# Sixteen modulation columns as one-column products on TensorE instead of VectorE reductions

## The chip, the core and the metric

The kernel runs on one core of one Trainium2 chip. The time is device microseconds of that core, as the median of three runs. In the profile PE is TensorE's matmuls, PEld its weight loads, DVE VectorE, ACT ScalarE, POOL GpSimd and SP the SyncE queue that issues the DMAs. Every engine works through its own instructions strictly in the order in which they stand there; a wait at the head of an engine's order holds everything behind it.

## The reference

Two layers and a large second block, on 512 tokens of 1024 features, all in fp32. What matters here is the modulation and the first layer, a convolution mixer:

```python
s_lat = jax.nn.silu(c)
for i in range(DEPTH):
    sh, sc, gt = jnp.split((s_lat @ w_mod[i] + b_mod[i])[:, None, :], 3, axis=-1)
    h = _rms(x, norm_g[i]) * (1.0 + sc) + sh
    ...
    x = x + gt * o

def _conv_mixer(h, w_in, dw, db, ln_g, ln_b, w_out):
    a, b, g = jnp.split(h @ w_in, 3, axis=-1)
    y = a * jax.nn.sigmoid(b)
    y = depthwise convolution of y with 31 taps + db
    y = jax.nn.silu(_layernorm(y, ln_g, ln_b)) * jax.nn.silu(g)
    return y @ w_out
```

The modulation is a product of one vector of 1024 numbers (silu of c) with matrices; the kernel makes 96 columns of 128 results of it. Columns 0 to 15 (shift and scale of layer 0) are needed before the first projection, 16 to 23 (its gate) and 24 to 31 (shift of layer 1) only after the convolution.

## The kernel before

x is kept feature-major: 8 chunks of 128 features by 512 tokens. Every large weight is split into hi + lo parts of a reduced fp32 type; a product of a 128x128 block with a chunk is three matmuls (`mm3`). Weights come in groups of 8 blocks (512 KB); for each group ScalarE casts hi (`whi`) and VectorE subtracts for lo (`wlo`, line 296).

The convolution stage runs from about 80 to 250 us. Its order on PE, ACT, DVE and POOL is written out by hand in the string `PLAN`: `l` is a chunk of the input projection (24 matmuls of 512 columns), `x` the sigmoid and product that follow it (VectorE makes the hi and lo tiles `e` for TensorE), `e` a step of the convolution on TensorE (12 matmuls of 256 columns with diagonals `dg`), `v` a step on VectorE (two operations, line 573), `p` a step on GpSimd (ScalarE multiplies by a tap, GpSimd adds), `b` makes diagonals (GpSimd, VectorE, or eight small ScalarE operations, line 525), `c` ends a chunk, and `g` is one column of the modulation. Chunks 0 and 2 are convolved on VectorE, 1 on GpSimd, 3 to 7 on TensorE.

A column is made by `gemv`: the 128x1024 slice `gw` comes by DMA into one of two buffers, and one VectorE operation (line 255) multiplies it by silu(c), which `cb` holds on every partition, and sums along the row into a column of `mod`; a small operation that reads the accumulator follows. The weight slice's buffer is free for the next DMA when VectorE has read it. PSUM banks of the pool `psr` (`pr()`, two banks) hold the last two results of the first projection (`r`), and later the mean and the statistics.

The first 16 columns are made before and during the first eight chunks of the projection (`lin_k`, until 79.7 us); the `g` of `PLAN` then make columns 16 onward, one after another.

Of the kernel before, what the change touches and what calls it, by code (L numbers as in the profile page):

```python
# [9 lines left out]
F32 = mybir.dt.float32  # L10
F32R = mybir.dt.float32r
AF = mybir.ActivationFunctionType
ALU = mybir.AluOpType

P = 128
T = 512
D = 1024
KC = D // P
# [11 lines left out]
# columns of the vector table  # L30
# [24 lines left out]
# how the work of the convolution is shared and ordered; with a count or a chunk, and the engines:  # L55
# l a chunk of the input projection, x what follows it, e v p a step of the convolution on TensorE, VectorE, GpSimd,
# b diagonals for TensorE's, c the end of a chunk, s a step of the statistics, z its norm, y its gate,
# m a source chunk of the output projection, g a column of the modulation
# [10 lines left out]
# steps of TensorE that a part of a stick-breaking head waits for the one before  # L69
# [20 lines left out]
# the projections of the stick-breaking heads in their order  # L90
# [3 lines left out]
def in2(name, i):  # L94
    """blocks of a part of the mixers' input projection"""
    if name == "v":
        return wide(SBV + 2 * i, 2)
    if name in "qk":
        return blocks_m_major(((SBQ if name == "q" else SBK) + i,), K8)
    if name == "rqk":  # L100
        return blocks_m_major((RQ + 2 * i, RQ + 2 * i + 1, RK + 2 * i, RK + 2 * i + 1), K8)
    if name == "rv":
        return wide(RV + 4 * i)
    if name == "rg":
        return blocks_m_major(range(RG + 4 * i, RG + 4 * i + 4), K8)
    return blocks_m_major(range(BRS, BRS + 16), K8)


# every block of every weight in the order of its use
# [17 lines left out]
# steps of TensorE at which a crossing emits its parts, per norm  # L127
# [4 lines left out]
def body(ctx: ExitStack, tc, ap, out):  # L132
    nc = tc.nc
# [15 lines left out]
    # working tiles of a phase, by tag  # L149
# [40 lines left out]
    # ---------------- constants  # L190
    vec = const.tile([P, NVEC], F32, name="vec")
    crow = gst.tile([P, D], F32, tag="g", name="crow")[0:1, :]
    ident = const.tile([P, P], F32, name="ident")
    x = []
    with tc.high_priority(offset=20000):
        for k in range(KC):
            t = const.tile([P, T], F32, name=nm("x"))
            nc.sync.dma_start(out=t, in_=ap["xt"][k])
            x.append(t)
            if k == 0:  # L200
                nc.sync.dma_start(out=crow, in_=ap["c"])
        nc.sync.dma_start(out=vec[:, 0:NHEAD], in_=ap["vec"][:, 0:NHEAD])
        nc.sync.dma_start(out=ident, in_=ap["cst"][:, 0:P])

# [20 lines left out]
    # 1 + b for the scales  # L225
    b1 = const.tile([P, 32], F32, name="b1")

    # mod columns: 0..23 layer 0 (shift, scale+1, gate), 24..47 layer 1, 48..95 second block
# [15 lines left out]
    def gemv():  # L244
        i = done[0]
        if i >= 96:
            return
        done[0] += 1
        if i == 48:
            cb.append(silu_c("c_2"))  # L250
        j = MOD_ORDER[i]
        with tc.high_priority(offset=3000):
            t = gst.tile([P, D], F32, tag="g", name=nm("gw"))
            nc.sync.dma_start(out=t, in_=ap["wmod"][j])
        product = V.tensor_tensor_reduce(  # L255
            out=t, in0=t, in1=cb[-1], scale=1.0, scalar=bias_of(j),
            op0=ALU.mult, op1=ALU.add, accum_out=mod[:, j:j + 1])
        tc.keep_in_program_order(product)
# [5 lines left out]
    # ---------------- weights  # L264
    at_block, loaded, fetched, groups, lead, ahead = [0], [0], [], {}, [LEAD], [0]

    def fetch(n):
        """ask for the groups up to the n-th"""
        while len(fetched) <= min(n, len(BLOCKS) // GB - 1):
            w = wst.tile([P, GB * P], F32, tag="w", name=nm("w"))  # L270
            with tc.high_priority(offset=3000):
                nc.sync.dma_start(out=w, in_=ap["weights"][len(fetched)])
            fetched.append(w)
# [6 lines left out]
    def group_steps(g, engs=None):  # L280
        """a group of blocks as hi + lo, with the next ones under way; a stop before lo"""
        while loaded[0] <= min(max(g, min(g + lead[0], at_block[0] // GB + 2)), len(BLOCKS) // GB - 1):
            n = loaded[0]
            loaded[0] += 1
            for _ in range(pace[0]):
                gemv()
            fetch(n + ahead[0])
            w, fetched[n] = fetched[n], None
            hi = wsp.tile([P, GB * P], F32R, tag="hi", name=nm("whi"))
            lo = wsp.tile([P, GB * P], F32R, tag="lo", name=nm("wlo"))  # L290
            A.copy(out=hi, in_=w)  # L291
            yield
            es = engs or (V if n else G,)
            for e, i in zip(es, range(0, GB * P, GB * P // len(es))):
                part = slice(i, i + GB * P // len(es))
                e.tensor_tensor(out=lo[:, part], in0=w[:, part], in1=f(hi[:, part]), op=ALU.subtract)  # L296
            groups[n] = hi, lo
            del w

    def block(i, n=1):  # L300
        """n blocks from the i-th after the current one"""
        g, r = divmod(at_block[0] + i, GB)
        hi, lo = group(g)
        return hi[:, r * P:(r + n) * P], lo[:, r * P:(r + n) * P]
# [15 lines left out]
    def lin(src, ms, kn, evac, halves=False, acc=acc):  # L320
        """feature-major products, one out-chunk after another"""
# [17 lines left out]
    def lin_k_steps(src, ms, kn, evac, banks=None):  # L339
        """k outermost, for sources that come one by one"""  # L340
# [24 lines left out]
    def split(src, scale=None, into=None, tag="a"):  # L365
        """PSUM as hi + lo"""
# [9 lines left out]
    def split_in(t, a=0, b=T, into=None, eng=None, n=T, tag="a"):  # L376
        """a tile as hi + lo"""
# [5 lines left out]
    # ---------------- statistics over features, per token  # L383
    class Stat:
        """sum of tiles"""
# [4 lines left out]
        def add(self, t):  # L390
            """the first tile is summed into"""
# [7 lines left out]
    def colsum(ps, c0, tiles, a, b, first=True, last=True):  # L399
        """ps[:, c0 + j] = sum over partitions and tiles of block j"""  # L400
# [5 lines left out]
    def bcast(ps, r, a, b):  # L406
        """ps[:, t] = r[t] on every partition; r has a token block in each column"""
# [3 lines left out]
    def rsqrt_steps(c, sq, n, a, b, rb, begun=False):  # L411
        """broadcast of 1/sqrt(mean + eps) into rb[:, a:b], with a stop before and after the root"""
# [10 lines left out]
    class Norm:  # L423
        """rms norm and modulation of x into split h, fed as chunks of x are updated"""
# [20 lines left out]
        def sum_half(self, m, a, b):  # L445
            """some tokens of a chunk into the sum"""
            V.tensor_tensor(out=self.sum.acc[:, a:b], in0=self.sum.acc[:, a:b], in1=self.tail[m][:, a:b], op=ALU.add)

        def sum_late(self):
            """all whole chunks into one sum"""  # L450
# [4 lines left out]
        def steps(self, a, b, early=False):  # L455
            """the statistics of some tokens"""
# [11 lines left out]
        def make_steps(self, k, a, b, pool=False):  # L468
            """a chunk of the result, with a stop before what waits for hi"""
# [18 lines left out]
        def makes(self, a, b):  # L488
            """all chunks, one after another"""
# [15 lines left out]
    # ================= first block, layer 0: convolution mixer  # L505
    # the taps of the chunks that TensorE convolves as hi | lo, and a diagonal per half of the partitions
# [10 lines left out]
    def diagonals(i, g, n, engs):  # L517
        """eight taps of 64 channels as hi and lo"""
# [44 lines left out]
    def conv_vector(chunks):  # L563
        """a tap of each chunk at a time"""
# [11 lines left out]
    def conv_pool(i):  # L576
        """a tap at a time"""
# [10 lines left out]
    def conv_tensor(i):  # L588
        """even and odd tokens of 64 channels on the two halves of the partitions, a few taps at a time"""
# [80 lines left out]
    def layer_stats():  # L670
        """mean and 1/sqrt(var + eps) of the convolved chunks, on every partition"""
# [49 lines left out]
    def crossing(which, src, ev, norm, half, free, *tiles):  # L721
        """the last two chunks of a residual and the first chunks of what follows its norm, by halves of the tokens"""
# [50 lines left out]
        # hi of a chunk, then its lo some chunks later; one result after another ends  # L773
# [25 lines left out]
    with tc.manual_schedule(engines=HAND):  # L799
# [33 lines left out]
        lead[0], ahead[0] = LEAD, 1  # L833
        engine = {"V": V, "A": A, "G": G}
# [38 lines left out]
    # ================= first block, layer 1: pooling mixer  # L873
# [7 lines left out]
    def pool_chunk(m, v):  # L881
        w = WINDOWS[m // 2]
        # running sums over aligned windows; v is padded by 8 in front and 8 behind
# [56 lines left out]
    # ================= second block: mixers  # L940
    h = n2.h
    # which score blocks share a PSUM bank: (block, offset, width)
# [5 lines left out]
    def lin_in(m):  # L948
        """one chunk of the mixers' input projection in two steps"""
# [8 lines left out]
    def sb_lin(w):  # L958
        i = int(w[1:])
        if w[0] == "v":  # L960
            # two pairs of heads, tokens on partitions: hi and lo of a head side by side
# [18 lines left out]
    # work that is emitted some steps of TensorE later  # L980
# [30 lines left out]
    def sb_q(i, o):  # L1011
        """per head hi and lo on the two halves of the partitions"""
# [7 lines left out]
    def sb_k(i, o):  # L1020
        """per head hi on both halves; lo of both heads"""
# [22 lines left out]
    def sb_scores(hd):  # L1044
# [20 lines left out]
        def softplus():  # L1065
            """softplus of the scores, summed over the later key blocks"""
# [61 lines left out]
    # retention: queries and keys of a head, chunk by chunk  # L1128
# [73 lines left out]
    # retention  # L1202
# [11 lines left out]
    def lin_tok():  # L1214
        """token-major products of 512 columns: four blocks of 128 tokens"""
# [77 lines left out]
    def ev_br(m, o, a, b):  # L1293
# [4 lines left out]
        else:  # L1298
            # all of the merged result but the last head
# [57 lines left out]
    # ================= feed-forward  # L1357
# [66 lines left out]


# ---- layout of the inputs
# [23 lines left out]
def taps_by_half(dw, db):  # L1450
    """taps and bias of the chunks that TensorE convolves, for even and odd tokens on the halves of the partitions"""
# [9 lines left out]
def arrays_of(i):  # L1461
# [4 lines left out]
    wm = np.concatenate([i["w_mod"][0].T, i["w_mod"][1].T, i["w_ada_2"][0].T], 0).reshape(96, P, D)  # L1466
    a["wmod"] = np.ascontiguousarray(wm)
# [30 lines left out]
```

## Time and profile before

| | us |
|---|---|
| runs, median of 3 | 1689.4 (1686.88 to 1690.16) |
| profiled execution, its span | 1686.7 |
| PE busy over the span | 1611.0 (96%) |
| DVE busy over the span | 1034.9 (61%) |
| ACT / POOL busy over the span | 596.0 / 500.8 |

The page gives no time of the profiled execution but its span; the median of the runs lies 2.7 us above it. Busy time is a share over stages with different limits: VectorE, at 61% of the whole, is in the convolution stage the busiest engine of all. A matmul's record is longer than its turn, since matmuls are pipelined; the distance from the start of one to the start of the next is what it costs in a row of them.

### The profile page before, as it was taken

The page shows a single profiled execution, that of the slowest core. Times are in us where ns is not written, and L with a number is a line of the kernel's source. Part 1 is how long each engine was busy: PE and PEld are TensorE (multiplying, and loading weights), DVE is VectorE, ACT ScalarE, POOL GpSimd, SP SyncE. Part 2 cuts the span into 40 slices and gives each one's busy share as a digit, 9 for nine tenths or more (in the row PEclk, how much of TensorE's full clock was granted, in tenths as well). Part 3 has the DMA queues.
Part 4 walks back from the last instruction along what each step waited for, and adds up shares of the span by engine and source line. Part 5 has one row for each costly group of instructions (what it writes and reads, how often), then busy time and mean ns, then how long its engine had stood idle before and what let it go on. Part 6 is the DMA issues. An engine that isn't in the chain of part 4 may idle for free.

```text
span 1686.7 us, 20261 instructions
## 1 busy us (share of the span) xinstructions
PE 1611.0 (96%) x7904; PEld 1347.1 (80%) x7904; DVE 1034.9 (61%) x1449; ACT 596.0 (35%) x920; POOL 500.8 (30%) x370
## 2 busy tenths in 40 slices
PE   6888899989999999999999999999999999999997
PEld 4677787867888878878888888888888888888887
DVE  6899987796677887886476554633254533333222
ACT  3422543513365556532332213223333422222221
POOL 2758645571124544460030200204441100000001
PEclk9999999999999999999999999999999999999999
DMA  7541334247521111225546332222322322332221
GB/s 266 168 150 64 113 126 147 74 148 250 187 76 51 60 53 51 70 66 158 175 144 201 99 119 75 94 89 75 99 91 84 100 90 99 100 100 90 98 92 58
DMA packets 54578, 187.64 MB, mean 111 GB/s; under 512 B 6097, under 2 KB 8273, under 8 KB 54482
## 3 DMA queue, kind: packets, MB, share of 16 engines
q1 hardware_dynamic: 52498, 183.20, 33.4%
q10 hardware_dynamic: 1984, 3.15, 0.6%
q8 instruction: 62, 1.02, 0.2%
q14 instruction: 34, 0.28, 0.1%
HBM read 184.22 MB, written 2.10 MB: 110 GB/s over the span
## 4 chain that ended last, share of the span: by engine, by line
PE 68%; DVE 18%; ACT 4%; issue 3%; DMA 3%; POOL 3%; SPq 0%; POOLq 0%; DVEq 0%; ACTq 0%
PE m L307 9%; PE m L309 9%; PE m L308 9%; PE z L309 7%; PE z L307 7%; PE z L308 7%; DVE wlo L296 4%; DVE gw L255 3%; DVE d L573 2%; DMA gw<-in_wmod 1%; DVE dg L527 1%; DMA w<-in_weights 1%; PE m L1222 1%; PE z L1222 1%; PE m L1224 1%
## 5 line engine op out<-in xcount | busy, mean ns | idle before, releaser
L296 DVE TENSOR_TENSOR wlo<-w,whi 128x1024 fp32r<-128x1024 f32 (+1 forms) x243 | 330.6, 1363 | 345.7 <-ACT whi L291 344.8
L291 ACT CAST whi<-w 128x1024 fp32r<-128x1024 f32 x244 | 255.2, 1049 | 633.2 <-PE m L308 269.9
L307 PE MATMUL m<-h,whi 128*128 128x512 f32 x730 | 287.4, 394 | 4.1 <-ACT a L644 2.0
L309 PE MATMUL m<-h,wlo 128*128 128x512 f32 x730 | 286.0, 392 | 3.5 <-DVE y L902 2.9
L308 PE MATMUL m<-h,whi 128*128 128x512 f32 x730 | 285.1, 391 | 1.9 <-POOL h L480 1.9
L309 PEld LDWEIGHTS m<-h,wlo 128*128 128x128 f32 x730 | 137.5, 188 | 34.1 <-DVE y L902 3.3
L307 PEld LDWEIGHTS m<-h,whi 128*128 128x128 f32 x730 | 137.9, 189 | 32.4 <-ACT a L644 2.2
L308 PEld LDWEIGHTS m<-h,whi 128*128 128x128 f32 x730 | 137.9, 189 | 29.8 <-POOL h L480 2.2
L309 PE MATMUL z<-h,wlo 128*128 128x512 f32 x338 | 133.0, 394 | 5.5 <-DVE y L902 5.4
L308 PE MATMUL z<-h,whi 128*128 128x512 f32 x338 | 132.8, 393 | 0.0
L307 PE MATMUL z<-h,whi 128*128 128x512 f32 x338 | 132.8, 393 | 0.0
L397 POOL TENSOR_TENSOR c<-c,c 128x512 f32<-128x512 f32 x10 | 13.4, 1337 | 372.9 <-ACT c L435 372.7
L397 POOL TENSOR_TENSOR s<-s,s 128x512 f32<-128x512 f32 x14 | 18.7, 1336 | 321.0 <-ACT s L1262 292.2
L255 DVE CUSTOM_DVE_ANT_0 gw<-gw,cb,vec 128x1024 f32<-128x1024 f32 x64 | 92.0, 1444 | 17.9 <-DMA gw<-in_wmod 11.4
L1041 POOL TENSOR_TENSOR s<-s,s 128x512 fp32r<-128x512 f32 x64 | 92.7, 1458 | 30.7 <-DVE s L1040 29.2
L309 PE MATMUL z<-a,wlo 128*128 128x512 f32 (+1 forms) x222 | 81.7, 368 | 1.5 <-DVE wlo L296 1.5
L307 PE MATMUL z<-a,whi 128*128 128x512 f32 (+1 forms) x222 | 82.1, 370 | 0.0
L308 PE MATMUL z<-a,whi 128*128 128x512 f32 (+1 forms) x222 | 81.5, 367 | 0.0
L309 PEld LDWEIGHTS z<-h,wlo 128*128 128x128 f32 x338 | 64.2, 190 | 20.2 <-DVE y L902 6.3
L308 PEld LDWEIGHTS z<-h,whi 128*128 128x128 f32 x338 | 64.0, 189 | 13.1
L307 PEld LDWEIGHTS z<-h,whi 128*128 128x128 f32 x338 | 64.1, 190 | 12.9
L307 PE MATMUL m<-a,whi 128*128 128x512 f32 (+1 forms) x196 | 71.5, 365 | 0.0
(415 smaller groups left out, 3540.2 us busy)
## 6 DMA issues: line engine op xcount, KB each, us to landing
w<-in_weights SPq DMA_DIRECT2D x244, 512.0 KB, 3.7
gw<-in_wmod SPq DMA_DIRECT2D x96, 512.0 KB, 4.2
x<-in_xt SPq DMA_DIRECT2D x8, 256.0 KB, 5.1
s<-in_dec ACTq DMA_DIRECT2D x4, 256.0 KB, 3.5
out_x<-h SPq DMA_DIRECT2D x4, 256.0 KB, 2.5
p<-in_cnt ACTq DMA_DIRECT2D x2, 256.0 KB, 2.7
v<-in_cnt ACTq DMA_DIRECT2D x2, 256.0 KB, 3.1
cb<-in_c SPq DMA_DIRECT2D x1, 512.0 KB, 6.1
```

Source lines behind the costliest of these rows:

```text
L255: product = V.tensor_tensor_reduce(out=t, in0=t, in1=cb[-1], scale=1.0, scalar=bias_of(j), op0=ALU.mult, op1=ALU.add, accum_out=mod[:, j:j ...
L291: A.copy(out=hi, in_=w)
L296: e.tensor_tensor(out=lo[:, part], in0=w[:, part], in1=f(hi[:, part]), op=ALU.subtract)
L307: mm(o, l[0], r[0], start=first, stop=False)
L308: mm(o, l[0], r[1], start=False, stop=False)
L309: mm(o, l[1], r[0], start=False, stop=last)
L397: self.eng.tensor_tensor(out=n, in0=self.acc, in1=t, op=ALU.add)
L527: engs[s].tensor_tensor(out=t.rearrange("p (a b) -> p a b", a=8), in0=diag.unsqueeze(1).to_broadcast([P, 8, P // 2]), in1=dws[s][:, c:c + ...
L573: V.scalar_tensor_tensor(out=cv[i], in0=y[:, j:j + T], scalar=tap(i, j), in1=cv[i], op0=ALU.mult, op1=ALU.add)
L1041: G.tensor_tensor(out=lo[:, 0:w], in0=t[:, 0:w], in1=f(hi[:, 0:w]), op=ALU.subtract)
L1222: mm(o, hh, wh, start=k == 0, stop=False)
L1224: mm(o, hl, wh, start=False, stop=k == KC - 1)
```

## The change

The slices of columns 16 to 31 are laid out anew in memory, so that a slice is eight 128x128 blocks with the input features on the partitions. Each of these columns is now eight fp32 matmuls of one moving column into a bank of `psr`, and a ScalarE operation that adds the bias and writes the column of `mod`. The vector c as a 128x8 tile (`ccol`) comes by one more DMA at the start, and ScalarE takes its silu after the first projection. The 16 VectorE reductions and their 16 accumulator reads fall away; the other 80 columns stay as they were.

```diff
+    ccol = const.tile([P, KC], F32, name="ccol")
...
         nc.sync.dma_start(out=ident, in_=ap["cst"][:, 0:P])
+        nc.sync.dma_start(out=ccol, in_=ap["ccol"])
...
     def gemv():
...
             nc.sync.dma_start(out=t, in_=ap["wmod"][j])
+        if j in MOD_ON_PE:
+
+            o = pr()
+            for k in range(KC):
+                mm(o[:, 0:1], t[:, k * P:(k + 1) * P], ccol[:, k:k + 1], start=k == 0, stop=k == KC - 1)
+            A.activation(out=mod[:, j:j + 1], in_=o[:, 0:1], func=AF.Identity, bias=bias_of(j))
+            return
         product = V.tensor_tensor_reduce(
...
         lin_k(h0, CV_FIRST, KC, ev_in)
         lead[0], ahead[0] = LEAD, 1
+        A.activation(out=ccol, in_=ccol, func=AF.Silu)
...
+MOD_ON_PE = set(range(16, 32))
...
+    a["ccol"] = np.ascontiguousarray(a["c"].reshape(KC, P).T)
+    for j in MOD_ON_PE:
+        wm[j] = wm[j].reshape(P, KC, P).transpose(2, 1, 0).reshape(P, D)
```

The orders of DVE, POOL and, apart from the new products, PE are the same as before; VectorE only loses 32 rows. On PE the place that matters first is the end of the first projection (`r` its last bank, `m` the bank of the next projected chunk). Before:

```order
L307 MATMUL r_233<-h_550,whi_521 128x512
L308 MATMUL r_233<-h_551,whi_521 128x512
L309 MATMUL r_233<-h_550,wlo_522 128x512
L307 MATMUL m_648<-h_206,whi_567 128x512
L308 MATMUL m_648<-h_207,whi_567 128x512
L309 MATMUL m_648<-h_206,wlo_568 128x512
```

And now, where each of the two new rows stands for eight products:

```order
L318 MATMUL r_235<-h_552,wlo_524 128x512
L261 MATMUL r_642<-ccol,gw_640 128x1 x8
L261 MATMUL r_659<-ccol,gw_657 128x1 x8
L316 MATMUL m_669<-h_208,whi_569 128x512
L317 MATMUL m_669<-h_209,whi_569 128x512
L318 MATMUL m_669<-h_208,wlo_570 128x512
```

The first two columns stand ahead of the first chunk of `PLAN`, and they read `ccol`.

On ACT the same place, from the last sigmoid of the first projection (`a<-r`) to the sigmoid of the chunk `m` (chunk 4, whose `e` tiles VectorE makes from it). Before:

```order
L644 ACTIVATE a_613<-r_233 128x512
L579 ACTIVATE v_640<-y_603,vec 128x512
L582 ACTIVATE p_642<-y_603,vec 128x512
L291 CAST whi_653<-w_649 128x1024
L291 CAST whi_659<-w_651 128x1024
L582 ACTIVATE p_715<-y_603,vec 128x512
L291 CAST whi_733<-w_657 128x1024
L582 ACTIVATE p_773<-y_603,vec 128x512
L644 ACTIVATE a_797<-m_648 128x512
```

And now:

```order
L653 ACTIVATE a_615<-r_235 128x512
L843 ACT_TABLE_LOAD
L843 ACTIVATE ccol<-ccol 128x8
L262 ACTIVATE mod<-r_642,vec 128x1
...
L262 ACTIVATE mod<-r_723,vec 128x1
L591 ACTIVATE p_745<-y_605,vec 128x512
L300 CAST whi_763<-w_678 128x1024
L591 ACTIVATE p_803<-y_605,vec 128x512
L262 ACTIVATE mod<-r_822,vec 128x1
L653 ACT_TABLE_LOAD
L653 ACTIVATE a_836<-m_669 128x512
```

Four columns' results, the silu of `ccol` and two loads of a function table now stand between the two sigmoids.

Further on, ACT where it changes to the table of the gates' silu and makes diagonals. Before:

```order
L582 ACTIVATE p_1669<-y_603,vec 128x512
L663 ACT_TABLE_LOAD
L663 ACTIVATE a_1675<-m_1510 128x512
L525 ACTIVATE dg_1679<-diag,a_139 128x64 x8
L663 ACTIVATE a_1702<-m_1634 128x512
L525 ACTIVATE dg_1716<-diag,a_138 128x64 x8
```

And now:

```order
L591 ACTIVATE p_1798<-y_605,vec 128x512
L262 ACTIVATE mod<-r_1803,vec 128x1
L672 ACT_TABLE_LOAD
L672 ACTIVATE a_1813<-m_1630 128x512
L534 ACTIVATE dg_1817<-diag,a_141 128x64 x8
L672 ACTIVATE a_1840<-m_1763 128x512
L534 ACTIVATE dg_1854<-diag,a_140 128x64 x8
```

The result of the 15th column (`r_1803`), which PE makes after the chunk `m_1763`, now stands ahead of the table load and the diagonals.

## Rows read from the trace of the kernel before

**Rows 1.** The page's span and busy times (share, instructions) of each engine.

```profile
span 1686.7 us, 20261 instructions
PE 1611.0 (96%) x7904; PEld 1347.1 (80%) x7904; DVE 1034.9 (61%) x1449; ACT 596.0 (35%) x920; POOL 500.8 (30%) x370
```

**Rows 2.** Stretch, length; busy time of each engine; granted clock, DMA share, GB/s.

```profile
79.70:249.80 170.10, 150.92 (x874) 133.29 (x874) 160.84 (x232) 65.05 (x135) 106.43 (x74) 0.96 0.33 107
249.80:302.00 52.20, 48.67 (x234) 39.95 (x232) 42.50 (x53) 21.77 (x32) 28.98 (x17) 0.97 0.45 152
```

**Rows 3.** PE's waits from 79 to 250 us: total, times, longest.

```profile
PE z L307 <- DVE dg L527: 14.5, 5, 5.5
PE m L307 <- ACT a L644: 2.0, 1, 2.0
PE z L309 <- DVE dg L527: 1.2, 1, 1.2
PE z L309 <- POOL dg L527: 0.5, 1, 0.5
PE z L308 <- DVE e L651: 0.5, 1, 0.5
```

**Rows 4.** The column operations on DVE, 85 to 232 us: ns min/median/max, or busy and mean.

```profile
L255 DVE CUSTOM_DVE_ANT_0 gw<-gw,cb,vec 128x1024 f32<-128x1024 f32 x16 | 25.4, 1598 | 1.4 <-DMA gw<-in_wmod 1.4
L255 DVE DVE_READ_ACCUMULATOR2_ANT mod<- x16: 73/77/85, 86.8 to 231.5; 128x1 f32 x16
```

**Rows 5.** Timeline of PE: first matmuls of two runs, and of what follows (start, us).

```profile
79.74 0.39 PE L307 MATMUL m<-h,whi 128*128 128x512 f32 x1
...
85.18 0.28 PE L307 MATMUL z<-e,a 128*128 128x256 f32 x1
...
89.49 0.39 PE L307 MATMUL m<-h,whi 128*128 128x512 f32 x1
```

**Rows 6.** PE's groups by shape, 79.7 to 249.8 us; a third of each kind.

```profile
L307 PE MATMUL m<-h,whi 128*128 128x512 f32 x120 | 47.3, 394 | 2.0 <-ACT a L644 2.0
L307 PE MATMUL z<-e,dg 128*128 128x256 f32 x128 | 38.9, 304 | 14.5 <-DVE dg L527 14.5
L307 PE MATMUL z<-e,a 128*128 128x256 f32 x32 | 9.0, 281 | 0.0
```

**Rows 7.** Timeline of PE around the one-column fp32 products of the statistics.

```profile
240.78 1.95 PE L404 MATMUL r<-ones,c 128*128 128x1 f32 x16 [0.18 <-DVE c L634]
242.58 0.48 PE L307 MATMUL m<-h,whi 128*128 128x512 f32 x1
```

**Rows 8.** Timeline of PE after two idle stretches, the second of 1.86 us.

```profile
74.51 0.63 PE L308 MATMUL z<-h,whi 128*128 128x512 f32 x1
74.93 0.63 PE L309 MATMUL z<-h,wlo 128*128 128x512 f32 x1
```

**Rows 9.** Timeline of ACT: sigmoids, a diagonal's eight parts, a table load with what follows.

```profile
79.94 0.60 ACT L644 ACTIVATE a<-r 128x512 f32<-128x512 f32 x1 [0.76 <-DVE y L902]
...
86.73 0.58 ACT L644 ACTIVATE a<-m 128x512 f32<-128x512 f32 x1
...
178.74 2.02 ACT L525 ACTIVATE dg<-diag,a 128x64 fp32r<-128x64 f32 x8 [1.45 <-PE z L308]
...
197.40 1.28 ACT L663 ACT_TABLE_LOAD   x1
198.70 0.60 ACT L663 ACTIVATE a<-m 128x512 f32<-128x512 f32 x1
```

**Rows 10.** Timeline of DVE: one set of chunk 4's `e` tiles; then a later set.

```profile
99.47 0.07 DVE L650 MEMSET e<- 128x8 f32 x1
...
101.84 1.47 DVE L380 TENSOR_TENSOR e<-e,e 128x272 fp32r<-128x272 f32 x1
...
137.43 0.07 DVE L650 MEMSET e<- 128x8 f32 x1
...
138.80 0.44 DVE L380 TENSOR_TENSOR e<-e,e 128x272 fp32r<-128x272 f32 x1
```

**Rows 11.** Timeline of SP: the DMA issue after which the new one stands.

```profile
5.80 0.33 SPq L203 DMA_DIRECT2D ident<-in_cst  x1
```

## The prediction

> **What bounds the kernel now.** I read the page first: over the whole span PE is 96% busy and DVE 61% [rows 1], which would say that work should never move towards PE. But these are averages, so the stage of the change is read by itself. In the stretch from the end of the first projection to the statistics' end, 170.1 us, DVE is busy 160.84 us and PE's records cover only 150.92 [rows 2]: here VectorE is the fullest engine, and the reader sees in PE's waits whom it waits for: 14.5 + 1.2 us for diagonals of DVE, 0.5 for its `e` tiles, 2.0 for a sigmoid of ACT, 0.5 for POOL, 18.7 us in five rows [rows 3]. After the stretch PE is full again: 48.67 of 52.2 us [rows 2].
>
> So the question is how much room PE has in these 170.1 us, in turns and not in records. 24 matmuls of 512 columns take from 79.74 to 85.18, that is 5.44 us or 0.227 each; 36 of 256 columns from 85.18 to 89.49, that is 4.31 us or 0.120 each [rows 5]. The stretch has 3 x 120 of the first kind and 3 x (128 + 32) of the second [rows 6]: 81.6 + 57.5 = 139.1 us. The statistics' sixteen records add 1.8 us [rows 7], and I allow 2.2 us for their broadcasts and one mean (17 records or so). PE's work is 143.1 us; 27.0 us of the stretch are open. 18.7 of them are the waits; the rest fits the granted clock's mean of 0.96 [rows 2]: 4% of 170.1 is 6.8 us. That loss looks like this: after an idle stretch the starts of 512-column matmuls stand 0.42 us apart instead of 0.227 [rows 8], TensorE's level of 1.2 instead of 2.4 GHz.
>
> **What the change removes.** 16 reductions, 25.4 us on DVE, and 16 accumulator reads of 0.077 us, 1.2 us [rows 4]: 26.6 us off VectorE. DVE's work in the stretch falls from 160.84 to about 134, well below PE's. So VectorE stops being the bound, and what it removes from the time is at most PE's waits.
>
> **What it adds on PE.** 16 columns of eight products. The same shape is in the trace: eight fp32 products with a 128x128 stationary block and one moving column stand there as 16 records from 240.78 to 242.58, 1.80 us [rows 7]. 16 x 1.80 = 28.8 us. They stand in PE's own order, so none of it is beside other PE work: 143.1 + 28.8 = 171.9 us, 1.8 us more than the stretch has now. **That is the step on which all hangs**: PE's open 27.0 us are used up by 28.8 us of new work, even if no wait at all were left.
>
> **What it adds in waits.**
> - *Start.* PE reaches the first column at 79.74 [rows 5], but that reads `ccol`, whose silu stands on ACT behind the last sigmoid, which runs from 79.94 to 80.54, and behind a table load. A load takes 1.28 us and what follows it starts 1.30 us after it began [rows 9]; for the silu of 8 columns I take 0.2 us (an eighth of a diagonal's 2.02 us is 0.25). 80.54 + 1.30 + 0.2 = 82.0: PE idles 2.3 us. Behind it stands the whole convolution.
> - *Chunk 4's tiles.* The sigmoid of chunk 4, now at 86.73 [rows 9], stands behind the results of four columns; the fourth is reached by PE only after the next projected chunk and five convolution steps. From its end: result 0.2, table load 1.3, sigmoid 0.6, then VectorE's first `e` set, which took 1.8 us at 137.43 and 3.8 at 99.47 [rows 10]: 3.9 to 5.9 us. PE has 36 matmuls of 256 columns in between, 4.3 us. Wait 0 to 1.6; I take 0.8. In the meantime VectorE, which is ahead, sits idle; what it gained by losing four reductions is spent there.
> - *The mean.* ScalarE's copy of the first convolved chunk now stands behind the sixth column's result, and PE's next matmul needs it: 0.2 + 0.6 = 0.8, rounded to 0.9 with the hand-over.
> - *Diagonals of ACT.* After the 15th column come result 0.2, load 1.3, sigmoid 0.6 and a diagonal of 2.0 [rows 9], 4.1 us, while PE has two steps of the convolution, 2.9 us: 1.2 us. The next sigmoid and diagonal, 2.6 us, stand against one step, 1.4: 1.1 us. Around the 12th to 14th columns the same pattern (result, diagonal of ACT, or VectorE's tiles behind a sigmoid) I put at 2.0. Together 4.3; bounds are 0, if ACT runs ahead, and 10, if each of the last eight columns costs the 1.2.
> - *The clock.* Fewer idle stretches than now: I keep half of the 6.8 us, 3.4; bounds 0 and 6.8.
>
> What I cost at nothing: the 16 result operations themselves (ACT is busy 65 of 170 us [rows 2]); GpSimd, whose taps wait for ACT a few us longer but whose diagonals PE needs later than now, too; the slices' DMAs, whose buffers are freed by PE instead of DVE at about the same places; and `ccol`'s DMA, one issue of 0.33 us [rows 11] ahead of the first slices (if nothing hid it, 0.3).
>
> Here a rule of the Trainium skill speaks against the change more than the row does. The row shows a table load of 1.28 us with the next operation 1.30 us after its start [rows 9]. The page "ScalarE: Activation LUTs", section "What ACT_TABLE_LOAD costs", states that a switch of sets also drains the engine for about 1.38 us, 2.66 us in all; by it the start and chunk 4's tiles would each be 1.4 us later, and the sum 2.8 us higher. The row has no such gap, so I go by the row.
>
> **The sum.** 1.8 + 2.3 + 0.8 + 0.9 + 4.3 + 3.4 = 13.5 us more at the end of the stretch. Behind it stand the layer norm and the output projection, which begin with PE's broadcasts and run as before; I see nothing that gives it back, since from there on PE is full. Against the profiled span of 1686.7 us that is 1700.2; the runs' median lies 2.7 above the span, so I take 1689.4 + 13 = 1702.4, rounded to **1702 us**.
>
> **Rivals.**
> - *It evens out.* ACT runs ahead, no wait is left and the clock stays up: +1.8 us, 1691. For it speaks that VectorE would have 36 us of air; against it that PE, ACT and DVE are now chained at each column. A change under 0.2% (3.4 us) can't be told from none here.
> - *Faster.* The columns cost PE less than the row says and slip into its waits. PE breaks even without waits at 27.0 / 16 = 1.69 us a column, with the waits above at (27.0 - 11.7) / 16 = 0.96. If a record took half its 0.113 us, 0.90 us a column: 143.1 + 14.4 = 157.5, 12.6 us under the stretch; with the waits above, 0.9 under it; between them 7 us, 1682. Against it stands the row itself, of the same shape and type.
> - *Lockstep.* Each result holds ACT until PE is there, ACT's sigmoids and taps come late, VectorE and GpSimd starve behind them, and PE goes on waiting for its diagonals as now: all 18.7 us and the clock's 6.8 stay, with the start's 2.3: 1.8 + 2.3 + 18.7 + 6.8 = 29.6 us, 1719. For it: chunk 4's sigmoid, with the fourth column ahead of it, comes some 20 us later by my count. Against it: later chunks' sigmoids stand well ahead of the steps that need them, and VectorE has 26.6 us less to do.
>
> **Numbers.** My forecast of a loss of 7 to 20 us, 1696 to 1709: 0.75. Evens out: 0.08. Faster: 0.04. Lockstep: 0.13. The range must leave out no more than 0.2: from 1693, which is near the even case, to 1712, within the lockstep. Slower by over 0.2%: the forecast and the lockstep, 0.88; same 0.08; faster 0.04.
>
> **What would show it.** Right: a column's 16 records take about 1.8 us on PE; PE's work and records in the stage fill it; its waits for VectorE's diagonals are nearly gone; a wait of some 2.3 us for ACT stands ahead of the first column; VectorE's idle time in the stage rises from 9 to over 40 us, much of it for ACT's sigmoids; the shift stands at the statistics and stays constant to the end. Wrong: columns much under 1.7 us; PE waits for VectorE that are as long as before; or a stage after 250 us that takes back what was lost.

## The result and the profile after

The change made the kernel slower: 1711.2 us, median of four runs (1705.9 to 1714.0), against 1689.8 of the kernel before (1686.9 to 1691.3). The ratio is 1.0123, 95% interval 1.0103 to 1.0143. The forecast was 1702, so the direction is right and the size 9 us short: the loss is 21.4 us where 13 were forecast. The execution below is the slowest of the four runs, with a span 25.5 us longer than the one before; the runs' medians differ by 21.4.

The page of the kernel after, its span and the busy times that answer to [rows 1]:

```profile
span 1712.2 us, 20764 instructions
PE 1650.8 (96%) x8160; PEld 1387.7 (81%) x8160; DVE 1001.2 (58%) x1417; ACT 601.7 (35%) x939; POOL 487.7 (28%) x370
```

PE's share is still 96%: an average over the span doesn't tell a loss from a gain here. The view of stretches does. Each row has the stretch, its length, the busy times of PE, weight loads, DVE, ACT and POOL, then the granted clock. The first row runs from the end of the first projection to the statistics and answers to [rows 2]; the others cut pieces from it.

```profile
79.00:262.90 183.90, 179.02 (x1076) 161.85 (x1075) 123.21 (x190) 68.73 (x150) 92.12 (x73) 0.92 0.28 92
...
80.00:90.00 10.00, 8.10 (x39) 7.43 (x40) 5.96 (x14) 5.20 (x8) 1.27 (x1) 0.69 0.32 103
...
120.00:130.00 10.00, 9.17 (x44) 8.05 (x44) 8.72 (x15) 3.68 (x7) 2.53 (x2) 0.57 0.31 107
130.00:140.00 10.00, 10.00 (x39) 9.13 (x40) 2.67 (x2) 2.12 (x5) 4.90 (x4) 0.50 0.36 111
```

The same stretch of the kernel before, up to its statistics, has this row:

```profile
79.50:240.80 161.30, 142.12 (x821) 125.42 (x819) 154.96 (x221) 61.66 (x130) 105.40 (x73) 0.96 0.31 99
```

So 22.6 of the 25.5 us arise here. PE's records now fill 179.0 of 183.9 us, and DVE, which was the fullest engine, is busy 123.2. But the granted clock fell from 0.96 to 0.92, and not evenly: from 130 to 140 us it is 0.50, that is 1.2 GHz all the time, while PE's records fill the whole 10 us. An engine that is "100% busy" at half speed looks the same in the busy column; only the clock column tells.

PE's waits in the stage (total, times, longest), which answer to [rows 3]:

```profile
PE r L261 <- ACT ccol L843: 2.2, 1, 2.2
PE r L619 <- ACT c L617: 0.8, 1, 0.8
PE z L317 <- DVE e L660: 0.8, 1, 0.8
PE z L316 <- ACT dg L534: 0.6, 1, 0.6
PE r L261 <- ACT mod L262: 0.4, 1, 0.4
PE z L316 <- DVE e L388: 0.2, 1, 0.2
```

The 14.5 us for VectorE's diagonals are gone, and all that PE waits for is 5.0 us. The others wait for PE and for each other instead; ACT's longest sum of waits and DVE's two longest are

```profile
ACT mod L262 <- PE r L261: 75.6, 14, 10.6
DVE wlo L305 <- ACT whi L300: 34.9, 9, 8.6
DVE e L662 <- ACT a L653: 17.8, 3, 10.3
```

PE's timeline at the first two columns, at the fifth and sixth, and at two later ones (start, duration, and in brackets the idle time before it and its releaser), beside [rows 5, 7, 8]:

```profile
81.55 1.95 PE L261 MATMUL r<-ccol,gw 128*128 128x1 f32 x16 [2.21 <-ACT ccol L843]
83.85 3.57 PE L261 MATMUL r<-ccol,gw 128*128 128x1 f32 x16 [0.35 <-ACT mod L262]
87.28 0.77 PE L316 MATMUL m<-h,whi 128*128 128x512 f32 x1
87.85 0.63 PE L317 MATMUL m<-h,whi 128*128 128x512 f32 x1
88.28 0.63 PE L318 MATMUL m<-h,wlo 128*128 128x512 f32 x1
...
117.80 3.63 PE L261 MATMUL r<-ccol,gw 128*128 128x1 f32 x32
122.26 2.07 PE L619 MATMUL r<-c,avg 128*128 128x512 f32 x2 [0.83 <-ACT c L617]
...
132.66 3.41 PE L261 MATMUL r<-ccol,gw 128*128 128x1 f32 x16
135.93 0.77 PE L316 MATMUL m<-h,whi 128*128 128x512 f32 x1
...
169.22 1.84 PE L261 MATMUL r<-ccol,gw 128*128 128x1 f32 x16
170.93 0.36 PE L316 MATMUL z<-e,dg 128*128 128x256 f32 x1
```

The length of a column is read from its start to the next start. At 169.22 it takes 1.71 us; at 132.66 it takes 3.27 and at 83.85 3.43, because the clock is at its lower level there, and the 512-column matmuls behind them stand 0.43 us apart instead of 0.227. The two columns from 117.80 (32 records, 3.63 us) are still fast. The granted clock is 1.00 from 121.0 to 121.4 us, where they end, and 0.52 from 121.4 to 122.2, in the mean's wait of 0.83 us; from there PE runs at the lower level until about 141.6, for some 20 us without another wait. A third fall, from about 199.9 to 203.4 us, has no wait ahead of it at all, only two more columns in a row (from 195.50).

The stage's ledger, kernel after against before: work 16 x 1.70 = +27.2; waits 18.7 to 5.0 = -13.7; clock, 4% of 161.3 to 8% of 183.9, 6.5 to 14.7 = +8.2. The sum is +21.7 of the 22.6 measured. The clock's terms are estimates: the mean clock also counts the time in which PE stands idle.

### The profile page after: what moved, and what is told of

It reads as the page before. It is cut to its first block, busy times and chain, and to the rows that moved or that the text cites. A ratio compares the mean times of both kernels' runs of the same rounds, so it can differ in the third digit from the quotient of the medians.

```text
span 1712.2 us, 20764 instructions
## 1 busy us (share of the span) xinstructions
PE 1650.8 (96%) x8160; PEld 1387.7 (81%) x8160; DVE 1001.2 (58%) x1417; ACT 601.7 (35%) x939; POOL 487.7 (28%) x370
## 4 chain that ended last, share of the span: by engine, by line
PE 77%; DVE 11%; ACT 4%; POOL 3%; issue 3%; DMA 2%; SPq 0%; POOLq 0%; DVEq 0%; ACTq 0%
PE m L316 11%; PE m L317 11%; PE m L318 11%; PE z L316 8%; PE z L318 8%; PE z L317 8%; DVE wlo L305 3%; PE r L261 2%; DVE gw L264 1%; DMA gw<-in_wmod 1%; PE m L1234 1%; PE z L1233 1%; PE z L1234 1%; PE m L1233 1%; PE m L1232 1%
## 5 line engine op out<-in xcount | busy, mean ns | idle before, releaser
L305 DVE TENSOR_TENSOR wlo<-w,whi 128x1024 fp32r<-128x1024 f32 (+1 forms) x243 | 325.3, 1341 | 379.8 <-ACT whi L300 378.8
L264 DVE CUSTOM_DVE_ANT_0 gw<-gw,cb,vec 128x1024 f32<-128x1024 f32 x48 | 66.6, 1394 | 14.3 <-ACT cb L213 7.1
```

Of the source, the lines that this page charges most:

```text
L264: product = V.tensor_tensor_reduce(out=t, in0=t, in1=cb[-1], scale=1.0, scalar=bias_of(j), op0=ALU.mult, op1=ALU.add, accum_out=mod[:, j:j ...
```

## The experiments

Two theories stood open on why the clock fell. **A**: products of one moving column bring TensorE's clock down, however close together they stand. **B**: the new stops of PE (for the silu, the results and the mean) bring it down, and the products are innocent. Beside both, **lockstep**: ACT, held by the columns' results, starves the others (later expectations call it theory C). All kernels were timed against the kernel before, with its median 1689.6 to 1689.8 in their batches. "Stage" is the time from the start of the first projection's last product to the statistics' first product in the profiled execution, with its granted clock; each is one execution, while the medians are over 4 to 12.

| kernel | median us (lowest to highest) | ratio [95%] | stage us | clock |
|---|---|---|---|---|
| before | 1689.8 | | 161.3 | 0.96 |
| after | 1711.2 (1705.9-1714.0) | 1.0123 [1.0103, 1.0143] | 184.0 | 0.92 |
| e1_wide | 1698.6 (1697.3-1699.1) | 1.0053 [1.0041, 1.0065] | 171.8 | 0.99 |
| e2_early | 1700.1 (1698.1-1703.5) | 1.0067 [1.0054, 1.0080] | 173.5 | 0.96 |
| e3_none | 1676.2 (1673.7-1678.8) | 0.9923 [0.9909, 0.9936] | 150.4 | 0.95 |
| e4_wide_early | 1695.7 (1693.2-1697.9) | 1.0038 [1.0024, 1.0051] | 167.9 | 1.00 |
| e5_eight_wide | 1683.7 (1680.6-1688.7) | 0.9969 [0.9956, 0.9982] | 157.5 | 1.00 |
| e6_eight_narrow | 1691.5 (1688.8-1697.5) | 1.0017 [1.0005, 1.0029] | 163.4 | 0.96 |
| e7_five_wide | 1691.4 (1689.7-1694.0) | 1.0011 [1.0003, 1.0019] | 164.3 | 0.96 |
| e8_both | 1700.5 (1698.9-1702.0) | 1.0063 [1.0050, 1.0075] | 174.0 | 0.99 |

**e1_wide: the same products with 128 moving columns.** The column of `ccol` is read 128 times over, and only the first result column is used.

```diff
-                mm(o[:, 0:1], t[:, k * P:(k + 1) * P], ccol[:, k:k + 1], start=k == 0, stop=k == KC - 1)
+                mm(o[:, 0:P], t[:, k * P:(k + 1) * P], ccol[:, k:k + 1].to_broadcast([P, P]), start=k == 0, stop=k == KC - 1)
```

> The changed kernel, but each of a column's eight products moves 128 columns (the same column of ccol repeated) instead of one; the result is read from the first. The trace of before has fp32 products with 128 moving columns at 0.106 us a record, the same as with one, so the length of the products stays at 1.7 us a column. Theory A (the one-column products themselves leave TensorE at 1.2 GHz): the granted clock in the convolution stage goes from 0.92 back to about 0.97, and 8 to 11 us of the 22 us lost there come back: 1700 to 1703 us. Theory B (the clock falls for the waits between engines alone): nothing changes, 1709 to 1713 us. If the wider products cost more per record than narrow ones, the time rises by that.

It measured 1698.6, 12.7 us less than the kernel after. PE's timeline and waits of e1_wide:

```profile
121.94 1.95 PE L261 MATMUL r<-ccol,gw 128*128 128x128 f32 x16
123.65 0.36 PE L316 MATMUL z<-e,dg 128*128 128x256 f32 x1
```

```profile
PE r L261 <- ACT ccol L843: 2.2, 1, 2.2
PE r L619 <- ACT c L617: 0.8, 1, 0.8
PE z L317 <- DVE e L660: 0.8, 1, 0.8
```

Its stretches at the start of the stage and behind the mean's wait:

```profile
80.00:90.00 10.00, 9.29 (x50) 8.58 (x51) 6.21 (x13) 4.36 (x8) 1.27 (x1) 0.83 0.37 113
...
120.00:140.00 20.00, 20.00 (x124) 17.77 (x123) 15.22 (x20) 8.23 (x13) 12.04 (x9) 1.00 0.39 130
```

A column takes 1.71 us as before, and the waits are the same to 0.1 us, but for the 0.4 behind the first column, which is gone. What differs is the clock: 1.00 from 120 to 140 us, where the kernel after had 0.57 and 0.50. The width is the only edit, and the granted clock of the whole execution is 0.987 to 0.989 in all five runs against 0.978 to 0.982 in the four of the kernel after. This is what A says, and 1.4 us more of a gain than A's range; B has no room for it, and lockstep, whose chain is untouched here, has none either. But waits have a part as well: behind the start's wait of 2.2 us the clock falls with wide columns too (0.83 from 80 to 90 us, 0.69 in the kernel after).

**e2_early: the silu of `ccol` ahead.** It stands at the start, behind the silu that is there already, with no table load of its own.

```diff
+            if k == 6:
+                A.activation(out=ccol, in_=ccol, func=AF.Silu)
...
-        A.activation(out=ccol, in_=ccol, func=AF.Silu)
```

> The changed kernel, but the silu of ccol is taken at the start of the program, behind the silu of c, so that no wait and no table load of it stands ahead of the first column; one of the two added loads before chunk 4's sigmoid is gone as well. Theory A: the start's wait of 2.2 us and about 1.3 us ahead of chunk 4's tiles go, the fall of the clock at the pair of columns stays: 3 to 5 us less, 1706 to 1709 us. Theory B: with the wait gone the clock does not fall at the start, and the 3 to 4 us at 1.2 GHz there go too: 6 to 9 us less, 1702 to 1705 us.

It measured 1700.1, 11.1 us less than the kernel after: more than either theory gave. Of the start's wait 0.7 us was left (for the last sigmoid). Its stretches, and the two columns behind which the last fall begins:

```profile
80.00:90.00 10.00, 9.65 (x47) 8.21 (x48) 5.46 (x11) 3.71 (x6) 1.27 (x1) 0.83 0.64 209
...
100.00:120.00 20.00, 19.17 (x141) 17.98 (x140) 13.00 (x22) 6.07 (x17) 7.09 (x6) 0.91 0.25 80
120.00:140.00 20.00, 20.00 (x129) 18.13 (x128) 13.69 (x18) 7.75 (x12) 12.27 (x9) 1.00 0.33 106
...
180.00:200.00 20.00, 20.00 (x125) 18.59 (x124) 13.42 (x22) 8.83 (x26) 8.90 (x9) 0.83 0.27 84
```

```profile
181.68 4.04 PE L261 MATMUL r<-ccol,gw 128*128 128x1 f32 x32
185.58 0.56 PE L316 MATMUL z<-e,dg 128*128 128x256 f32 x1
```

The clock still falls in three places, each behind one-column products, and in the last of them PE has no idle time at all (20.00 of 20 us), so stops alone don't explain it: the two columns take 3.90 us instead of twice 1.70, because the clock falls within them. But the long fall behind the mean's wait has become a short one (some 3.5 us): from 120 to 140 us the clock is 1.00, with the same two columns and the same wait of 0.8 us ahead. Why that fall lasted 20 us in the kernel after is not settled; neither theory says how long a fall lasts, and both ranges were missed.

**e3_none: what the relief of VectorE is worth.** Columns 16 to 31 are not computed at all (`mod` is zero there), while their slices are still loaded.

> Columns 16 to 31 are not computed at all (their places in mod are zero; the slices are still loaded): VectorE's relief of 26.6 us alone, without anything on PE or ACT. If PE's waits for VectorE were worth what the rows say (18.7 us and the clock's 6.8), the convolution stage ends 15 to 25 us sooner than before: 1665 to 1675 us. If the stage is held by something else (ACT's and GpSimd's chain), it gains under 8 us: over 1682 us.

It measured 1676.2, 13.5 us under before and just above what was expected. PE's waits for VectorE in the stage of e3_none:

```profile
PE z L319 <- DVE dg L539: 7.9, 3, 4.9
PE z L321 <- DVE dg L539: 0.9, 1, 0.9
```

With 26.6 us taken off VectorE, PE still waits 8.8 us for its diagonals, against 15.7 in [rows 3]. The relief alone brings 13.5 us, half of the 27.2 that the columns cost PE.

**e4_wide_early: both edits, e1_wide's and e2_early's.**

> Both edits: 128 moving columns and the early silu. Theory A: the gains add, 1696 to 1700 us; the floor by PE's work is 1691 us. Theory B: like the early silu alone, 1702 to 1705 us.

1695.7, with the clock at 1.00 over the whole stage: just under A's range (which added the gains), far from B's, and 6 us above before. That is the price of sixteen columns on PE with the clock out of the account. The two edits, worth 12.7 and 11.1 us singly, bring 15.5 together, so their gains don't add: they remove largely the same loss.

Where two columns stand in a row, the traces can be set side by side. The kernel after and e2_early have three such places each, and within or behind all six the clock falls. e1_wide, e4_wide_early and e8_both (below) have the same places with wide products, and of these nine only one is followed by a fall: the first of e1_wide, behind the start's wait of 2.2 us.

**e5_eight_wide and e6_eight_narrow: every second column.** Both have the early silu and `MOD_ON_PE = set(range(16, 32, 2))`, so that no two columns stand in a row; VectorE makes the other eight. e5 has 128 moving columns, e6 one.

> Only every second one of the sixteen columns (eight in all) is made on TensorE, with 128 moving columns and the silu of ccol taken at the start; the other eight stay on VectorE. By the balance of the stage PE then has 143 + 8 x 1.7 = 157 us of turns and VectorE 161 - 8 x 1.66 = 148 us, both under the 170 us of before. Theory A (the bound is PE's turns, plus the clock): the stage ends 3 to 8 us sooner than before, 1682 to 1687 us. Theory C (the columns' results on ACT chain the engines so that VectorE's relief is lost): no faster than before, 1689 to 1694 us.

> The same eight columns with one moving column as in the change; no two of them stand next to each other. If single narrow columns are harmless and only two in a row bring the clock down: within 2 us of the wide one. If each narrow column pulls the clock down: 4 to 8 us slower than the wide one.

e5 took 1683.7 us and beats both kernels; e6 took 1691.5. All nine runs of e5 (at most 1688.7) lie under all twelve of e6 (at least 1688.8), and the width is the only difference. PE's waits in the stage are the same rows in both, 2.7, 2.0, 0.7 and 0.6 us. PE's timeline of e5_eight_wide at the mean and at its longest wait:

```profile
108.75 1.95 PE L261 MATMUL r<-ccol,gw 128*128 128x128 f32 x16
112.74 1.12 PE L619 MATMUL r<-c,avg 128*128 128x512 f32 x2 [2.04 <-ACT c L617]
...
164.47 0.39 PE L316 MATMUL z<-e,dg 128*128 128x256 f32 x1 [2.67 <-DVE dg L536]
...
166.37 1.95 PE L261 MATMUL r<-ccol,gw 128*128 128x128 f32 x16
```

and of e6_eight_narrow at the same places of the program:

```profile
109.91 1.84 PE L261 MATMUL r<-ccol,gw 128*128 128x1 f32 x16
113.79 2.08 PE L619 MATMUL r<-c,avg 128*128 128x512 f32 x2 [2.05 <-ACT c L617]
...
167.09 0.39 PE L316 MATMUL z<-e,dg 128*128 128x256 f32 x1 [2.67 <-DVE dg L536]
...
168.27 0.42 PE L316 MATMUL z<-e,dg 128*128 128x256 f32 x1
168.48 0.42 PE L317 MATMUL z<-e,dg 128*128 128x256 f32 x1
...
169.55 3.41 PE L261 MATMUL r<-ccol,gw 128*128 128x1 f32 x16
```

e5 stays at 2.4 GHz throughout the stage. In e6 the clock falls twice. At the mean, a narrow column stands just ahead of the wait of 2.05 us, and PE runs at 1.2 GHz behind it until about 117; in e5 a wide one stands there and the clock stays up. At the longest wait, e6 is at 1.2 GHz from 168.27 until 178, and this fall begins before its column does; the narrow column ahead of it lies 16 us earlier (151.32). So this second fall can't be laid on the width of a neighbouring column. Waits of this length go either way without one, too: in the kernel before, 2.28 us ahead of 204.25 are followed by no fall (1.00 from 200 to 210 us), while in e3_none, which has no columns on PE, 1.79 us ahead of 193.44 are (0.91 from 180 to 200 us). That eight narrow columns cost 7.8 us is shown by the runs; that the first fall is its column's work rests on one place in one execution, and what decides the second is open. Of the 25 single narrow columns that begin at 2.4 GHz in the kernel after, e2_early and e6, only the one at e6's mean is followed by a fall.

The Trainium skill, "TensorE: Matmul & The Clock Gate", section "The HAM clock gate", names idleness of TensorE as what lowers the clock. The trace agrees for e6's fall behind the wait of 2.67 us; in e2_early's third fall there is no idle time (20.00 of 20 us), so here narrow products count beside it.

Where e5's gain over the kernel before comes from can be added up as for the kernel after: work 8 x 1.70 = +13.6; waits 18.7 to 6.0 = -12.7; clock 6.5 to 0 = -6.5. That is -5.6; the stage is 3.8 us shorter. Work against waits alone is about even, and e6, which has these two terms without the clock's, is no faster than before.

**e7_five_wide: five columns, {21, 23, 25, 27, 29}, wide and early.**

> Five columns (21, 23, 25, 27, 29) on TensorE, wide, silu at the start, none of them at the beginning of the stage or ahead of chunk 4's sigmoid. PE 151.5 us, VectorE 152.5 us of turns: the best balance by the sums. Theory A: 2 to 7 us under before, 1683 to 1688 us. Theory C: no faster than before.

1691.4: a miss for theory A. The number is the one that theory C gave, but the trace shows another reason. PE's longest wait in e7_five_wide, and the column behind it:

```profile
PE r L261 <- DMA gw<-in_wmod: 6.5, 1, 6.5
```

```profile
115.30 3.75 PE L261 MATMUL r<-ccol,gw 128*128 128x128 f32 x16 [6.48 <-DMA gw<-in_wmod]
118.71 0.77 PE L316 MATMUL m<-h,whi 128*128 128x512 f32 x1
```

The wait of the DMA queue from 110 to 113 us:

```profile
SPq L256 <- DVE mod L264: 7.1, 1, 7.1
```

A column on PE makes PE wait for its slice's DMA, which on VectorE cost only VectorE's time; and after such a stop even wide products run at the lower clock (3.41 us). The slice came late because its DMA was issued late: the two buffers are shared by both kinds of column, and the queue waited 7.1 us for a column on VectorE, which ran only from 110.31 to 111.52, behind 8 us of convolution steps. The issue followed at 111.63, the data landed some 3.6 us later, and PE began at 115.30. No run removes this wait.

**e8_both: the columns on PE, but VectorE's sixteen kept.** PE makes sixteen wide columns from blocks of `x` with the early silu, and ScalarE writes them to a tile that nothing reads; `mod` comes from VectorE as before.

```diff
...
-                mm(o[:, 0:1], t[:, k * P:(k + 1) * P], ccol[:, k:k + 1], start=k == 0, stop=k == KC - 1)
-            A.activation(out=mod[:, j:j + 1], in_=o[:, 0:1], func=AF.Identity, bias=bias_of(j))
-            return
+                mm(o[:, 0:P], x[k][:, 0:P], ccol[:, k:k + 1].to_broadcast([P, P]), start=k == 0, stop=k == KC - 1)
+            A.activation(out=mod2[:, j - 16:j - 15], in_=o[:, 0:1], func=AF.Identity, bias=bias_of(j))
...
```

> VectorE keeps all sixteen reductions as in the kernel before, and PE makes sixteen columns' worth of products all the same (128 moving columns, silu at the start, on blocks of x that are there already, into columns that nothing uses): the added work on PE and ACT without any relief of VectorE. If PE's turns alone set the stage (theory A), VectorE's relief is worth little and this comes out near the one with wide columns and early silu, 1695 to 1700 us. If the relief counts and PE then waits for VectorE as before on top of its new work, 1706 to 1716 us.

1700.5, just above the range that theory A gave, 4.7 us over e4_wide_early. PE's wait for VectorE's diagonals is 3.7 us, not 14.5 as in [rows 3]: with 27 us more to do, PE arrives later at them by itself. Behind the longer of these waits (2.9 us) the clock falls once (0.91 from 200 to 220 us), with wide products. So the same relief of VectorE is worth 13.5 us while PE has room (e3_none) and 4.7 us once PE carries the products.

## Why the prediction was right, and short

The direction and what bounds the stage were right. That 1711.2 lies inside the range is in part luck: it is above the 1696 to 1709 of the forecast itself, which had 0.75, and 0.8 us under the upper end, which was put at 1712, within the lockstep. And one large error, the clock, was partly made up by smaller ones the other way.

- **What bounds the stage: right.** PE's room of 27.0 us is used up by the columns; with the clock at 1.00 sixteen of them still cost 6 us (e4_wide_early).
- **A column's price: 1.80 forecast, 1.70 measured,** from the statistics' sixteen records [rows 7]. Over 16 columns that is 1.6 us less: the term +1.8 was +0.2.
- **The waits: right in place, too high in sum.** Start 2.3 forecast, 2.2 measured. Chunk 4's tiles 0.8 and 1.0 (0.8 + 0.2). The mean 0.9 and 0.8. The diagonals of ACT 4.3 and 0.6: ScalarE got ahead there, towards the lower bound of 0. Not foreseen: 0.4 for the first column's result. In all 5.0 instead of 8.3 (each rounded). The table load on which the first two terms rest went as [rows 9] said:

```profile
80.00 1.28 ACT L843 ACT_TABLE_LOAD   x1
81.29 0.21 ACT L843 ACTIVATE ccol<-ccol 128x8 f32<-128x8 f32 x1
```

  The silu starts 1.29 us after the load. The 1.38 us of draining that the Trainium skill's page "ScalarE: Activation LUTs", section "What ACT_TABLE_LOAD costs", adds to a switch are not seen here.
- **The clock: the step that failed.** "Fewer idle stretches than now: I keep half of the 6.8 us, 3.4; bounds 0 and 6.8." It measured 14.7 in the stage, outside the bounds. The step took idle time alone for the cause, and so let a stage with fewer waits have a better clock. e1_wide against the kernel after, and e5 against e6, show that one-column products lower the clock at equal waits, by 12.7 us for sixteen and 7.8 us for eight. Widening alone takes the 14.7 to some 1.7 us (1% of 171.8), so the narrow products have a part in nearly all of it. But the early silu alone takes it to some 6.9 (4% of 173.5), with all products narrow: how far waits beside them, or the time at which they come, are needed is not separated, and why they lower the clock stays open. This one term is 11.3 us too low; the others together 4.9 us too high. With both put right the sum of 13.5 is 19.9 of the 22.6 us measured. Of the rest, 1.5 us was open in the prediction already: 27.0 less 18.7 is 8.3, not the 6.8 that it gave to the clock. (The sum was also added to the median as 13, not 13.5.)
- **Nothing given back: right.** From the statistics to the end the profiled execution even lost 3.4 us more (1686.7 - 240.8 = 1445.9 before, 1712.2 - 262.9 = 1449.3 after). Most of it lies in this stretch, first before, then after:

```profile
480.00:640.00 160.00, 157.20 (x884) 131.75 (x884) 127.54 (x210) 92.11 (x171) 67.07 (x58) 1.00 0.18 57
```

```profile
502.00:665.50 163.50, 160.71 (x882) 134.93 (x882) 126.99 (x210) 92.05 (x171) 66.62 (x58) 0.97 0.17 55
```

  It is clock again, on work that the change doesn't touch. It is one execution, and the kernel's runs lie 8 us apart; whether it belongs to the change is open.
- **The rivals.** Lockstep's chain exists: ACT waits 75.6 us for PE and VectorE over 50 for ACT. But PE hardly waits for them, so it isn't what costs; its 1719 rested on 18.7 us of waits staying, and 5.0 were left. The sign "idle time of VectorE over 40 us" came, with 60.7 (183.9 - 123.2), but only 17.8 of it for ACT's sigmoids and 34.9 for its casts of weights. "Evens out" failed by the clock, and with the clock up sixteen columns are still 6 us above before (e4_wide_early). "Faster" put the break-even at 1.69 us a column without waits; 1.70 was measured, so sixteen could not win. Eight do (e5_eight_wide, 6 us under before): with half the work PE's waits fall by 12.7 us, nearly the 13.7 that they fall by in the kernel after, and the clock at 1.00 makes a gain of it.

## What to carry to other kernels

Work moved to an engine with room is worth its relief only up to where that engine becomes the bound: count the room in turns, then move less than fills it. That alone is no gain yet: here half the columns won when they were wide (1683.7) and not when they were narrow (1691.5), and five wide ones, with a late DMA among their waits, did not win either (1691.4). When thin matmuls enter a dense stream, read the granted clock by stretches before the waits: a stage can be full of PE records and be at half speed. If the clock falls behind one-column products, try to widen them with a broadcast operand: here it cost nothing (1.71 us a column either way) and brought the stage's clock from 0.92 to 0.99.

## What the hardware showed that was not expected

- Eight fp32 products with a 128x128 stationary block take 1.71 us as 16 records with one moving column and 1.71 us with 128 (the kernel after at 169.22, e1_wide at 121.94). The width is free there, as was expected for e1_wide.
- Yet the granted clock of the stage is 0.92 with one column and 0.99 with 128, with the same waits; with eight columns it is 0.96 and 1.00. Each is one execution; the runs' medians (12.7 and 7.8 us apart) agree.
- In e2_early the clock was 0.83 from 180 to 200 us although PE's records fill every microsecond of it: a fall without a stop, behind two columns in a row. The wide pair at the same place of e4_wide_early (from 181.29) leaves it at 1.00.
